# Last norm: the variance ahead of all but one subtraction, its sums in halves, and the last states' evictions as chains of their own

## The chip, the cores and the metric

The kernel runs on one core of a Trainium2 chip. The metric is the device time of one execution in microseconds, the median of several runs. Five engines work side by side, each through its own instructions in order: TensorE (PE, with its weight loads shown as PEld), VectorE (DVE), ScalarE (ACT), GpSimd (POOL) and SyncE (SP), which here only issues DMAs. They wait for each other through semaphores.

## The reference

One inference step of a decoder layer for 256 prompt tokens and 64 sample tokens (8 sequences of 8), 320 in all. Two token mixers run on the same input, their outputs are merged and projected, and two norms close the two halves of the layer:

```python
def _layernorm(x, g, b):
    mu = jnp.mean(xf, axis=-1, keepdims=True)
    var = jnp.mean(jnp.square(xf - mu), axis=-1, keepdims=True)
    return (xf - mu) * lax.rsqrt(var + LN_EPS) * g + b

x1 = LayerNorm(alpha * x + W_out(sig(g_a) * A(x) W_a + sig(g_b) * B(x) W_b))
y  = LayerNorm(alpha * x1 + relu(x1 W_up)^2 W_down)

C_new = decay * C + einsum('bhs,bhsk,bhsv->bhkv', w_end, k, v)      # mLSTM, 4 heads, 256 x 512
S_new = exp(G_end) * S + einsum('bhsk,bhsv->bhkv', k * exp(G_end - G), i)   # HGRN2, 8 heads, 128 x 256
```

The outputs are y and the new states. All is float32. The change touches the second norm (the one that gives y) and the last states of the prompt: C (4 heads, two blocks of 128x512 each) and S (8 heads, 128x256 each).

## The kernel before

Features lie on the partitions, in 16 blocks of 128, and the 320 tokens on the free axis. The whole layer is a list of 307 weight tiles of 2048 x 128. A tile is worked in two units of eight 128x128 weight blocks. Full precision is made from rounded numbers (float32r): a weight block w is split by ScalarE into a rounded half (`wh`) and by VectorE into the rest (`wl`), the moving operand likewise, and three matmuls hi*hi, hi*lo and lo*hi are accumulated, so a unit is 24 matmuls. Raw weights are loaded by SP into three buffers. The split halves have pairs of buffers: three narrow ones (`wh`, `wl`) and, from the output projection on, five wide ones in the tile `bb` (`wx[0]` to `wx[4]`). `prep` (L469) splits the next unit whenever a pair is free, and `give` (L544) hands a pair back when its unit is through; near the end it hands them to the last states' loads instead (`vx` for V halves, `kx` for K halves, loaded by GpSimd in `m_C`).

The order of the instructions on each engine is fixed when the program is built. Beside the main loop over weight tiles, each piece of side work is a chain: a Python generator that yields one operation at a time, with an estimated cost. A scheduler (`Sched`) keeps an estimated time for each engine. After each group of three matmuls it goes through all chains in order of rank (0 is first) and issues what its estimate says is ready, on the engine that the chain names. `wait` holds a chain for an event, `post` sets one, `acq` and `rel` take and return a buffer. Chips do not see these estimates: they only see the order that results.

The end of the program:

- The last 16 tiles (`dn`, f = 3) give the 16 blocks of the second norm's input; `ev_dn` (L1910) adds each to the residual in `acc` (the tile `f3m`). From block 4 on, a provisional mean `cb` of the first four blocks is subtracted first, so `ln_add` (L1722) waits for that mean after block 3.
- `ln_sum` keeps two sums over blocks, of z and of its square, one 128x320 tile each. The sum over the partitions is a matmul with a matrix of ones. In the first norm it is done by `total` (L1768), on halves that lie in the wide buffer `wx[4]` (`lns`, L606), which L1761 then returns to the weights. In the second norm it is a full-precision matmul: one after block 3, two after block 14 (`ln_pre`), two for block 15 itself (`ln_final`).
- `ln_scale` (L1807) gives the mean M, its square T, the variance X (L1816, L1819), logarithm and exponential, and a Newton step (L1822 to L1824).
- `y` (L1930) subtracts M from all 16 blocks (L1938) and multiplies them by the inverse deviation (L1943) on VectorE; `yb_` scales each by g and adds b on ScalarE, and stores blocks in pairs.
- `m_C` (L1098) and `h_S` (L1569) compute the C blocks and S heads on TensorE after the last tile. VectorE or ScalarE evicts them from PSUM (`oC`, `oS`), and SP stores them. They are chains of rank 3, and the eviction and store of a block belong to the chain that makes its sums.

Of the kernel before, what the change touches and what calls it, by code (L numbers as in the profile page):

```python
# [256 lines left out]
def post(ev):  # L257
    return ("set", ev)
# [47 lines left out]
class Program:  # L306
# [791 lines left out]
    def m_C(self, h):  # L1098
        k = yield acq(self.kx)
        kt = yield ("pool", 1000, lambda: self.nc.gpsimd.dma_start(k, self.kD[h]))  # L1100
        w = yield acq(self.vx)
        vt = yield ("pool", 1000, lambda: self.nc.gpsimd.dma_start(w, self.vD[h]))
        e = Ev()
        e.t = max(kt, vt) + 4000.0
        yield wait(e, self.main_end)
        for c in range(2):
            if h:
                yield wait(self.ln[1]["fin"])
            b = yield acq(self.mbank)
            yield ("pe", 6 * pe_r(512), lambda: [self.mm(  # L1110
                b, k[:, x, s, 128 * c:128 * c + 128], w[:, y, s, :], start=n == 0, stop=n == 5)
                for n, (s, x, y) in enumerate((s, x, y) for s in range(2) for x, y in ((0, 0), (0, 1), (1, 0)))])
            if c == 1:
                yield post(self.mh[h]["C"])
            if h < 2 and c == 0:
                yield ("dve", dve(512, True), lambda: self.nc.vector.tensor_copy(self.oC[h][:, c, :], b))
            else:
                yield ("act", act(512, True), lambda: self.A(self.oC[h][:, c, :], b))
            yield rel(self.mbank, b)
            yield ("sp", 620, lambda: self.dma(self.d["Cp"][h, :, c, :], self.oC[h][:, c, :]))  # L1120
        yield rel(self.vx, w)

# [446 lines left out]
    def h_S(self, h):  # L1569
# [7 lines left out]
            b[:, 0:256], x[:, 128 * i:128 * i + 128], x[:, 256 + 256 * i:512 + 256 * i], start=i == 0, stop=i == 1) for i in range(2)])  # L1577
        if h < 4:
            yield ("act", act(256, True), lambda: self.A(self.oS[:, h, :], b[:, 0:256]))
        else:  # L1580
            yield ("dve", dve(256, True), lambda: self.nc.vector.tensor_copy(self.oS[:, h, :], b[:, 0:256]))
# [140 lines left out]
    def ln_add(self, n, j, z, pre):  # L1722
# [4 lines left out]
        if j < 4:  # L1727
# [7 lines left out]
            if j == 3:  # L1735
                p = yield acq(self.sbank)
                if n == 0:
                    yield from self.total(p, S1, self.lns[0])
                else:
                    yield ("pe", pe_f(TOK), lambda: self.mm(p[:, :TOK], self.ones, S1, start=True, stop=True))  # L1740
# [16 lines left out]
        if j == 15:  # L1757
# [3 lines left out]
            self.hl_free.append((self.s.t["pe"], self.wx[4]))  # L1761
# [6 lines left out]
    def total(self, p, x, hl):  # L1768
        hi, lo = hl[:, 0, :], hl[:, 1, :]
        yield from self.split(x, hi, lo)  # L1770
        for i, y in enumerate((hi, lo)):
            yield ("pe", 147, lambda: self.mm(p[:, :TOK], self.ones.bitcast(F32R), y, start=i == 0, stop=i == 1))
# [14 lines left out]
    def ln_pre(self, n):  # L1787

        p = self.ln[n]["p"] = yield acq(self.sbank, 2)
        for i in range(2):  # L1790
            yield ("pe", pe_f(TOK), lambda: self.mm(p[i][:, :TOK], self.ones, self.lnb[i], start=True, stop=False))
# [15 lines left out]
    def ln_scale(self, n):  # L1807
# [11 lines left out]
        yield ("dve", dve(TOK, mode=2), lambda: v.tensor_scalar(X, X, 0.0, EPS, ALU.max, ALU.add))  # L1819
        yield ("act", act(TOK), lambda: self.A(RS, X, AF.Ln))  # L1820
# [109 lines left out]
    def y(self):  # L1930
# [4 lines left out]
        for i in range(KT + 6):  # L1935
# [3 lines left out]
            if i == 5:  # L1939
                yield wait(st["end"])  # L1940
            if i > 5:
                z = self.acc[:, i - 6, :]
                t = yield ("dve", dve(TOK), lambda: v.tensor_tensor(z, z, self.lnb[4], ALU.mult), (0.0,))  # L1943
                self.s.spawn(self.yb_(i - 6, z), 0, t)
# [9 lines left out]
    def run(self, pool):  # L1954
# [12 lines left out]
        self.ln = [dict(c=Ev(), end=Ev(), pre=Ev(), m=Ev(), fin=Ev(), s=[Ev() for _ in range(KT)]) for _ in range(2)]  # L1967
# [83 lines left out]
```

## Time and profile before

| | |
|---|---|
| median of 3 runs | 2321.09 us (2320.81 to 2322.24) |
| the profiled execution | 2321.41 us, span 2319.6 us |
| last accumulation of block 15 (L1918) | 2292.21 us from the span's start |
| ScalarE's last scaling of y ends | 2313.49 us |
| granted TensorE clock, mean | 0.999 |

The page gives the busy time of each engine in one profiled execution, and the trace behind it the start and length of each instruction. A row of the timeline is: start, length, engine, line, operation, out<-in, shapes and count, and in brackets how long the engine stood idle before it and what released it. The length of an operation is longer than its engine is occupied, since the next one can start before it ends: what an operation occupies is read from the starts. The line of a helper stands for all that it issues (L342 is every ScalarE operation, L348 nearly every matmul, L351 SP's DMAs), so one goes by the names of the tiles.

### The profile page before, as it was taken

How to read it: one execution, taken by the hardware profiler on the slowest of the kernel's cores; microseconds unless marked ns; L12 is line 12 of the kernel's file. 1: busy time of each engine (PE TensorE's matmuls, PEld its weight loads, DVE VectorE, ACT ScalarE, POOL GpSimd, SP SyncE). 2: the span in 40 equal slices, each digit the busy share in tenths (PEclk: the TensorE clock that was granted, in tenths of full speed). 3: DMA queues.
4: the chain of work that ended last, by engine and by line, in shares of the span. 5: the costliest groups of instructions: out<-in, count | busy, mean ns of one | idle time of the engine just before them, and what ended most of it. 6: DMA issues, size and time to landing. Idle time of an engine off the chain costs nothing.

```text
span 2319.6 us, 38982 instructions
## 1 busy us (share of the span) xinstructions
PE 2309.1 (100%) x15808; PEld 2267.0 (98%) x15808; DVE 1351.6 (58%) x2297; ACT 1059.5 (46%) x1703; POOL 11.9 (1%) x37
## 2 busy tenths in 40 slices
PE   9999999999999999999999999999999999999998
PEld 9999999999999999999999999999999999999997
DVE  6566567666666776555555767654444444444455
ACT  5444445555556565444433446533442343234333
POOL 0000000000000000000000000000000000000000
PEclk9999999999999999999999999999999999999999
DMA  7676777555555555555545654444444444444465
GB/s 282 206 254 223 269 280 230 193 187 181 183 181 188 182 189 172 174 177 169 176 169 176 213 167 152 150 146 154 146 155 146 154 147 154 146 153 147 153 219 182
DMA packets 143275, 424.92 MB, mean 183 GB/s; under 512 B 16372, under 2 KB 37748, under 8 KB 142072
## 3 DMA queue, kind: packets, MB, share of 16 engines
q1 hardware_dynamic: 141800, 415.96, 53.9%
q0 software_dynamic: 1152, 6.29, 0.8%
q8 instruction: 123, 2.02, 0.4%
q14 instruction: 56, 0.46, 0.1%
q10 hardware_dynamic: 144, 0.20, 0.0%
HBM read 371.48 MB, written 50.90 MB: 182 GB/s over the span
## 4 chain that ended last, share of the span: by engine, by line
PE 98%; ACT 1%; DVE 0%; DMA 0%; issue 0%; SPq 0%; ACTq 0%; DVEq 0%
PE bank L348 97%; ACT f3m L342 0%; DMA f<-first 0%; PE bank L1610 0%; PE bank L946 0%; PE bank L1175 0%; PE bank L1448 0%; DVE f3m L1938 0%; ACT f L342 0%; PE bank L1453 0%; PE bank L1019 0%; PE bank L1502 0%; PE bank L993 0%; PE bank L1559 0%; ACT oC L342 0%
## 5 line engine op out<-in xcount | busy, mean ns | idle before, releaser
L348 PE MATMUL bank<-xh,wh 128*128 128x320 f32 (+1 forms) x2432 | 782.4, 322 | 0.3 <-ACT wh L342 0.3
L488 DVE TENSOR_TENSOR wl<-wr,wh 128x1024 fp32r<-128x1024 f32 x426 | 522.0, 1225 | 399.6 <-ACT wh L342 395.9
L348 PE MATMUL bank<-xh,wl 128*128 128x320 f32 (+1 forms) x2432 | 752.2, 310 | 0.0
L348 PE MATMUL bank<-xl,wh 128*128 128x320 f32 (+1 forms) x2432 | 749.8, 309 | 0.0
L342 ACT ACTIVATE wh<-wr 128x1024 fp32r<-128x1024 f32 x426 | 451.0, 1059 | 498.1 <-PE bank L348 478.2
L348 PEld LDWEIGHTS bank<-xh,wh 128*128 128x128 f32 x2432 | 457.8, 188 | 19.2 <-issue 14.7
L348 PEld LDWEIGHTS bank<-xl,wh 128*128 128x128 f32 x2432 | 458.1, 189 | 2.9
L348 PEld LDWEIGHTS bank<-xh,wl 128*128 128x128 f32 x2432 | 458.0, 188 | 0.5 <-DVE wl L701 0.3
L488 DVE TENSOR_TENSOR bb<-wr,bb 128x1024 fp32r<-128x1024 f32 x176 | 215.7, 1226 | 229.2 <-ACT bb L342 229.1
L342 ACT ACTIVATE bb<-wr 128x1024 fp32r<-128x1024 f32 x176 | 186.4, 1059 | 313.3 <-PE bank L348 294.9
L348 PE MATMUL bank<-xh,bb 128*128 128x320 f32 (+1 forms) x1280 | 285.4, 309 | 0.0
L348 PE MATMUL bank<-rxb,bb 128*128 128x320 f32 x1208 | 276.3, 309 | 0.0
L348 PE MATMUL bank<-ra,wh 128*128 128x320 f32 x988 | 265.9, 308 | 0.0
L348 PE MATMUL bank<-ra,bb 128*128 128x320 f32 x1096 | 264.2, 308 | 0.7 <-DVE ra L1640 0.7
L348 PEld LDWEIGHTS bank<-xh,bb 128*128 128x128 f32 x1280 | 215.0, 188 | 0.0
L348 PEld LDWEIGHTS bank<-rxb,bb 128*128 128x128 f32 x1208 | 204.3, 188 | 0.2
L348 PE MATMUL bank<-xl,bb 128*128 128x320 f32 (+1 forms) x640 | 197.7, 309 | 0.0
L348 PEld LDWEIGHTS bank<-ra,bb 128*128 128x128 f32 x1096 | 187.1, 188 | 1.2 <-DVE ra L1640 0.9
L348 PEld LDWEIGHTS bank<-ra,wh 128*128 128x128 f32 x988 | 176.3, 188 | 0.0
L348 PE MATMUL bank<-rxb,wh 128*128 128x320 f32 x548 | 169.0, 308 | 0.0
L348 PE MATMUL bank<-rxb,wl 128*128 128x320 f32 x548 | 169.0, 308 | 0.0
L348 PEld LDWEIGHTS bank<-xl,bb 128*128 128x128 f32 x640 | 120.4, 188 | 0.3 <-DVE xl L1863 0.3
(263 smaller groups left out, 2233.9 us busy)
## 6 DMA issues: line engine op xcount, KB each, us to landing
wr<-wt SPq DMA_DIRECT2D x602, 512.0 KB, 3.4
rx<-C SPq DMA_DIRECT2D x34, 256.0 KB, 5.6
Cs<-rx SPq DMA_DIRECT2D x34, 256.0 KB, 4.4
f<-C SPq DMA_DIRECT2D x30, 256.0 KB, 5.3
Cs<-f SPq DMA_DIRECT2D x30, 256.0 KB, 4.8
f<-first SPq DMA_DIRECT2D x6, 704.0 KB, 10.8
vD<-ra SPq DMA_DIRECT2D x4, 1024.0 KB, 6.8
f<-S SPq DMA_DIRECT2D x8, 512.0 KB, 6.6
```

Source lines behind the costliest of these rows:

```text
L342: return self.nc.scalar.activation(out, in_, func, **kw)
L348: self.nc.tensor.matmul(*a, **kw)
L488: self.V().tensor_tensor(lo, raw, hi.bitcast(F32), ALU.subtract)
```

## The change

It does five things. (1) The second norm's sums over partitions go through `total`, in halves, where the sum can be made before block 15: one after block 3, two after block 14. `ln_final`'s two stay as they were. (2) For that, `wx[4]` is no longer returned after the first norm. (3) In `y`, VectorE subtracts from block 0 only, then waits for a new event `x` (the variance is made), subtracts from blocks 1 and 2, waits for the inverse deviation, and then alternates; before, it subtracted from six blocks ahead of that last wait, and nothing held the variance in front of them. (4) The eviction and store of each C block and S head become a chain of rank 0, spawned after its matmuls. (5) All C blocks are evicted by ScalarE; before, VectorE evicted the first blocks of heads 0 and 1. The second block of head 0 now waits for `fin` as well.

```diff
         for c in range(2):
-            if h:
+            if h or c:
                 yield wait(self.ln[1]["fin"])
...
-            if h < 2 and c == 0:
-                yield ("dve", dve(512, True), lambda: self.nc.vector.tensor_copy(self.oC[h][:, c, :], b))
-            else:
-                yield ("act", act(512, True), lambda: self.A(self.oC[h][:, c, :], b))
-            yield rel(self.mbank, b)
-            yield ("sp", 620, lambda: self.dma(self.d["Cp"][h, :, c, :], self.oC[h][:, c, :]))
+            self.s.spawn(self.C_out(h, c, b), 0, self.s.t["pe"])
         yield rel(self.vx, w)
+
+    def C_out(self, h, c, b):
+
+        yield ("act", act(512, True), lambda: self.A(self.oC[h][:, c, :], b))
+        yield rel(self.mbank, b)
+        yield ("sp", 620, lambda: self.dma(self.d["Cp"][h, :, c, :], self.oC[h][:, c, :]))
...
+        self.s.spawn(self.S_out(h, b), 0, self.s.t["pe"])
+
+    def S_out(self, h, b):
...
-                if n == 0:
-                    yield from self.total(p, S1, self.lns[0])
-                else:
-                    yield ("pe", pe_f(TOK), lambda: self.mm(p[:, :TOK], self.ones, S1, start=True, stop=True))
+                yield from self.total(p, S1, self.lns[0])
...
-            self.hl_free.append((self.s.t["pe"], self.wx[4]))
...
-    def total(self, p, x, hl):
+    def total(self, p, x, hl, stop=True):
         hi, lo = hl[:, 0, :], hl[:, 1, :]
         yield from self.split(x, hi, lo)
         for i, y in enumerate((hi, lo)):
-            yield ("pe", 147, lambda: self.mm(p[:, :TOK], self.ones.bitcast(F32R), y, start=i == 0, stop=i == 1))
+            yield ("pe", 147, lambda: self.mm(p[:, :TOK], self.ones.bitcast(F32R), y, start=i == 0, stop=stop and i == 1))
...
-            yield ("pe", pe_f(TOK), lambda: self.mm(p[i][:, :TOK], self.ones, self.lnb[i], start=True, stop=False))
+            yield from self.total(p[i], self.lnb[i], self.lns[1 + i], False)
...
         yield ("dve", dve(TOK, mode=2), lambda: v.tensor_scalar(X, X, 0.0, EPS, ALU.max, ALU.add))
+        if n:
+            yield post(st["x"])
...
-        for i in range(KT + 6):
+        for i in range(KT + 3):
...
-            if i == 5:
+            if i == 0:
+                yield wait(st["x"])
+            elif i == 2:
                 yield wait(st["end"])
-            if i > 5:
-                z = self.acc[:, i - 6, :]
+            if i > 2:
+                z = self.acc[:, i - 3, :]
                 t = yield ("dve", dve(TOK), lambda: v.tensor_tensor(z, z, self.lnb[4], ALU.mult), (0.0,))
-                self.s.spawn(self.yb_(i - 6, z), 0, t)
+                self.s.spawn(self.yb_(i - 3, z), 0, t)
```

What this does to the order is seen on three places. The first is VectorE behind the last accumulation into `f3m` (L1918 before, L1921 after), up to the first product. Names: `f_76` holds the norm's small tiles (M, T, X and the inverse deviation), `bank_87` and `bank_85` are C blocks, `bank_88` is the sum of squares. Before:

```order
L1918 TENSOR_TENSOR f3m<-f3m,bank_81 128x320
L1116 COPY oC<-bank_87 128x512
L1938 TENSOR_TENSOR f3m<-f3m,f_76 128x320 x6
L1816 SCALAR_TENSOR_TENSOR f_76<-bank_88,f_76 128x320
L1819 TENSOR_SCALAR f_76<-f_76 128x320
L1822 SCALAR_TENSOR_TENSOR f_76<-f_76 128x320
L1116 COPY oC<-bank_85 128x512
L1823 TENSOR_TENSOR f_76<-f_76 128x320
L1824 SCALAR_TENSOR_TENSOR f_76<-f_76 128x320
L1938 TENSOR_TENSOR f3m<-f3m,f_76 128x320
L1943 TENSOR_TENSOR f3m<-f3m,f_76 128x320
```

After:

```order
L1921 TENSOR_TENSOR f3m<-f3m,bank_81 128x320
L1941 TENSOR_TENSOR f3m<-f3m,f_76 128x320
L1817 SCALAR_TENSOR_TENSOR f_76<-bank_88,f_76 128x320
L1820 TENSOR_SCALAR f_76<-f_76 128x320
L1941 TENSOR_TENSOR f3m<-f3m,f_76 128x320 x2
L1825 SCALAR_TENSOR_TENSOR f_76<-f_76 128x320
L1826 TENSOR_TENSOR f_76<-f_76 128x320
L1827 SCALAR_TENSOR_TENSOR f_76<-f_76 128x320
L1941 TENSOR_TENSOR f3m<-f3m,f_76 128x320
L1948 TENSOR_TENSOR f3m<-f3m,f_76 128x320
```

The variance stands behind one subtraction instead of six and two copies of C are gone, one of them from between the Newton steps; three of the subtractions that stood in front now stand among the products.

The second place is ScalarE in the same stretch, from the square of block 15 to the first scalings of y (`f3m<-f3m,vec`). `bank_86` is the sum of z. Before:

```order
L342 ACTIVATE f_76<-f3m 128x320 x3
L342 ACTIVATE f_76<-bank_86 128x320 x2
L342 ACTIVATE oC<-bank_84 128x512
L342 ACTIVATE f_76<-f_76 128x320 x2
L342 ACTIVATE oC<-bank_82 128x512
L342 ACTIVATE oC<-bank_83 128x512
L342 ACTIVATE f3m<-f3m,vec 128x320 x2
L342 ACTIVATE oC<-bank_81 128x512
```

After:

```order
L342 ACTIVATE f_76<-f3m 128x320
L342 ACTIVATE oC<-bank_87 128x512
L342 ACTIVATE f_76<-bank_86 128x320 x2
L342 ACTIVATE f_76<-f_76 128x320
L342 ACTIVATE oC<-bank_84 128x512
L342 ACTIVATE f_76<-f_76 128x320
L342 ACTIVATE oC<-bank_85 128x512
L342 ACTIVATE oC<-bank_82 128x512
L342 ACTIVATE f3m<-f3m,vec 128x320
L342 ACTIVATE oC<-bank_81 128x512
```

Here `f_76<-bank_86 x2` are M and T, and `f_76<-f_76` are logarithm and exponential. The first C block is evicted ahead of M, and the second has moved from in front of the logarithm to between logarithm and exponential. After the first scaling four C evictions follow, before it were three.

The third place is VectorE in the last two tiles, where the last weights are prepared (L488) and blocks 13 and 14 accumulated (L1918 or L1921). Before:

```order
L488 TENSOR_TENSOR bb<-wr,bb 128x1024
L1918 TENSOR_TENSOR f3m<-f3m,bank_82 128x320
L1783 TENSOR_TENSOR f_76<-f_76,f3m 128x320
L1784 TENSOR_TENSOR f_76<-f_76 128x320
L1916 TENSOR_TENSOR f3m<-f3m,f_76 128x320
L1918 TENSOR_TENSOR f3m<-f3m,bank_83 128x320
L1783 TENSOR_TENSOR f_76<-f_76,f3m 128x320
L1784 TENSOR_TENSOR f_76<-f_76 128x320
L1916 TENSOR_TENSOR f3m<-f3m,f_76 128x320
```

After:

```order
L1921 TENSOR_TENSOR f3m<-f3m,bank_82 128x320
L1784 TENSOR_TENSOR f_76<-f_76,f3m 128x320
L1785 TENSOR_TENSOR f_76<-f_76 128x320
L488 TENSOR_TENSOR bb<-wr,bb 128x1024
L1919 TENSOR_TENSOR f3m<-f3m,f_76 128x320
L1921 TENSOR_TENSOR f3m<-f3m,bank_83 128x320
L1784 TENSOR_TENSOR f_76<-f_76,f3m 128x320
L1785 TENSOR_TENSOR f_76<-f_76 128x320
L1645 TENSOR_TENSOR bb<-f_76,bb 128x320 x2
L1919 TENSOR_TENSOR f3m<-f3m,f_76 128x320
```

The last unit's weights are prepared one tile later, behind the accumulation of block 13, and the rests of the two sums' halves (L1645) follow block 14.

More of the change, by code (lines that the diff above doesn't have):

```diff
@@ L1966, in run @@
         self.vD = [self.dr.tile([128, 2, 2, 512], F32, name=f"vD{j}") for j in range(MH)]
-        self.ln = [dict(c=Ev(), end=Ev(), pre=Ev(), m=Ev(), fin=Ev(), s=[Ev() for _ in range(KT)]) for _ in range(2)]
+        self.ln = [dict(c=Ev(), end=Ev(), pre=Ev(), m=Ev(), fin=Ev(), x=Ev(), s=[Ev() for _ in range(KT)]) for _ in range(2)]
         self.xq, self.xq_ev = [None] * KT, [Ev() for _ in range(KT)]
```

## The prediction

> **What bounds the kernel now.** I read the busy times first, then the waits of TensorE's own queue, then the chain that ended last, and only then the last 30 us in order of time.
>
> ```profile
> span 2319.6 us, 38982 instructions
> PE 2309.1 (100%) x15808; PEld 2267.0 (98%) x15808; DVE 1351.6 (58%) x2297; ACT 1059.5 (46%) x1703; POOL 11.9 (1%) x37
> ...
> PE bank L348 <- DVE ra L1640: 0.7, 1, 0.7
> PE bank L348 <- ACT wh L342: 0.3, 1, 0.3
> ```
>
> TensorE is busy from end to end; between the start and the last weight tile it waits 0.7 and 0.3 us. Up to there only TensorE's own work counts, and VectorE and ScalarE have room. The tail is another program: there TensorE's remaining sums are short, and the chain of waits runs through VectorE and ScalarE.
>
> ```profile
> 2295.02 2.09 DVE f3m L1938 x5
> 2297.11 0.41 DVE f L1816
> ...
> 2297.91 0.48 ACT f L342
> ...
> 2298.91 0.49 DVE f L1822
> 2299.41 0.60 DVE oC L1116
> ...
> 2301.33 0.40 DVE f3m L1943
> ...
> 2302.57 0.66 ACT f3m L342
> 2303.23 0.48 ACT oC L342
> ...
> 2308.05 0.54 ACT oS L342 x2
> ...
> 2312.40 1.09 ACT f3m L342 x2
> ```
>
> The columns are the start, the length and what. From 2295.02 five subtractions of the mean (L1938, behind a first one) stand ahead of the variance (L1816); logarithm, exponential and three small VectorE steps follow, with one copy of a C block (L1116) among them; the first product (L1943) comes at 2301.33. From 2302.57 ScalarE is never idle until 2313.49: 15 scalings of y, 3 evictions of C and 4 of S, which is 10.92 us. Behind it lie the stores.
>
> ```profile
> 2308.08 0.33 SPq L351 DMA_DIRECT2D y<-f3m  x1
> ...
> 2313.51 0.62 SPq L351 DMA_DIRECT2D y<-f3m  x1
> 2314.22 0.98 SPq L351 DMA_DIRECT2D Sp<-oS  x2
> SPq L2047 <- DMA Sp<-oS: 2.6, 1, 2.6
> 2308.00:2309.00 1.00, 1.00 (x6) 0.88 (x5) 1.00 (x4) 1.00 (x4) 0.00 (x0) 1.00 0.24 90
> 2309.00:2310.00 1.00, 1.00 (x6) 0.89 (x5) 1.00 (x3) 1.00 (x3) 0.00 (x0) 1.00 1.01 385
> 2314.00:2316.00 2.00, 0.00 (x0) 0.00 (x0) 0.00 (x0) 0.00 (x0) 0.00 (x0) 0.91 1.03 362
> 2317.00:2318.00 1.00, 0.00 (x0) 0.00 (x0) 0.00 (x0) 0.00 (x0) 0.00 (x0) 0.50 0.17 57
> ```
>
> The last store is issued at about 2314.7 and waited for 2.6 us. The last two columns of the stretches are the DMA share and GB/s: nearly idle in 2308 to 2309, then full from 2309 until, at 57 against 362 GB/s, the stream ends in the first sixth of 2317 to 2318, about 2317.2. The store issued at 2308.08 filled the engines from 2309.0 on, 0.9 behind its issue. So the end is ScalarE's last scaling, two issues, and a backlog of stores that began late. Everything is worked out on this execution, 2321.41 us (span 2319.6 and 1.8 around it); the median of the three runs is 0.3 lower.
>
> **The sums in halves.** Three full-precision sums of the last norm become a rounded half and a rest, two matmuls instead of one.
>
> ```profile
> 2209.29 0.31 PE L348 MATMUL bank<-rxb,bb 128*128 128x320 f32 x1
> 2209.44 0.70 PE L348 MATMUL bank<-f,ones 128*128 128x320 f32 x2
> ...
> 2210.12 0.31 PE L348 MATMUL bank<-ra,bb 128*128 128x320 f32 x1
> 1394.31 0.31 PE L348 MATMUL bank<-bb,ones 128*128 128x320 f32 x1
> 1394.46 0.31 PE L348 MATMUL bank<-xh,bb 128*128 128x322 f32 x1
> ```
>
> Matmuls are pipelined, so starts are what counts. A half occupies 0.15 (1394.31 to 1394.46, in the first norm). From 2209.29 to 2210.12, 0.83, pass two ordinary matmuls (0.30) and one full-precision sum: 0.53. Each sum therefore saves 0.53 - 0.30 = 0.23, three save 0.7 us, straight off the main stretch. The splits, three ScalarE and three VectorE operations of 0.5 each, cost nothing: two pairs lie in the last tile, where these rows show the cover, and the third in the middle of the stage.
>
> ```profile
> 2276.96 1.06 ACT L342 ACTIVATE bb<-wr 128x1024 fp32r<-128x1024 f32 x1 [2.46 <-PE bank L348]
> 2278.05 1.23 DVE L488 TENSOR_TENSOR bb<-wr,bb 128x1024 fp32r<-128x1024 f32 x1 [1.89 <-ACT bb L342]
> 2284.10 0.49 DVE L1918 TENSOR_TENSOR f3m<-f3m,bank 128x320 f32<-128x320 f32 x1 [2.99 <-PE bank L348]
> 2292.21 0.49 DVE L1918 TENSOR_TENSOR f3m<-f3m,bank 128x320 f32<-128x320 f32 x1 [6.14 <-PE bank L348]
> ```
>
> Ahead of the last accumulation VectorE idles 6.14 us; without that cover the two pairs would add their 2.0. The halves take buffer 4 of the wide weight buffers for good, so weights rotate through seven instead of eight pairs, and through three instead of four in the last nine units. A unit is 24 matmuls of 0.147, 3.5 us; its preparation runs from 2276.96 (the release) to 2279.28, 2.3 us, and about 0.3 for handovers. With three pairs a buffer is refilled two units, 7.1, ahead of use: 4.5 us of slack. In the last tile the only VectorE wait in front is the accumulation at 2284.10, and in the new order the last preparation stands ahead of it. I cost this at nothing; unhidden it is a unit's preparation, 2.6, per stall. The fourth V halves also now wait for the very last unit's buffer.
>
> ```profile
> 2288.41 0.54 POOL L1102 DMA_DIRECT2D bb<-vD  x1 [6.13 <-PE bank L348]
> DMA to landing us min/median/max: 5.2/7.6/9.7
> 2301.33 1.52 PE L348 MATMUL bank<-bb,wh 128*128 128x512 f32 x6
> ```
>
> Issued at about 2292.2 in place of 2288.41, they land between 2297.4 and 2301.9; the matmuls that read them start at 2301.33. On the median there are 1.5 us to spare; at worst 0.6 is lost, off the path since the last S copies have more than that. Zero.
>
> **The variance ahead of the subtractions.** All times here are on the old clock, before the 0.7. The variance needs the square of the mean and one subtraction now goes in front.
>
> ```profile
> 2293.60 0.69 DVE L1116 COPY oC<-bank 128x512 f32<-128x512 f32 x1 [0.90 <-PE bank L348]
> 2294.14 0.77 ACT L342 ACTIVATE f<-bank 128x320 f32<-128x320 f32 x2 [0.87 <-PE bank L348]
> 2296.07 0.60 ACT L342 ACTIVATE oC<-bank 128x512 f32<-128x512 f32 x1 [1.16 <-PE bank L348]
> 2308.49 2.90 DVE L1943 TENSOR_TENSOR f3m<-f3m,f 128x320 f32<-128x320 f32 x7
> 2309.22 1.89 PE L348 MATMUL bank<-xls 128*128 128x256 f32 x8
> 2311.30 1.41 DVE L1581 COPY oS<-bank 128x256 f32<-128x256 f32 x4
> ```
>
> Mean and square are done at 2294.91, so the variance starts at 2295.02 instead of 2297.11, 2.09 earlier; the logarithm, 0.80 behind it as before, at 2295.82, ending 2296.30. There the new order puts an eviction of C before the exponential. Its sums are done by 2296.07, so it does not wait, and it occupies ScalarE 0.48: the exponential ends at 2297.26 and L1822's step starts at 2297.28 instead of 2298.91, 1.63 earlier. The copy of 0.60 between the three steps is gone. Together 2.23: the first product at 2299.1, the first scaling at 2299.6. If that eviction had to wait, or the copy's place was idle anyway, 1.5 would remain. The new waits of the chains (for `x`, for `fin`) hold nothing else up: they set VectorE's order, shown above, and TensorE's order of the tail stays, but for two banks that change places.
>
> VectorE then has 13 subtractions and 16 products instead of 10 and 16. Its pitch is 0.40: the first product starts at 2301.3, the tenth, first of the last seven, at 2308.49, eighteen operations later. The three extra subtractions take back 1.2, and the last product starts near 2309.9; the four S copies behind it, 0.35 each (1.41/4), end near 2311.8, the last of them behind TensorE's last S sum at 2311.1 (2309.22 + 1.89).
>
> **Evictions.** The first C block is evicted by ScalarE before the mean: its sums end at 2293.60, where the copy on VectorE starts now; 0.48 later ScalarE is free at 2294.08, and the mean waits for TensorE until 2294.14. Nothing. After the first scaling stand 15 scalings, four C evictions (one more) and four S: 10.92 + 0.48 = 11.40, behind the first one's 0.55 (1.09/2), from 2299.6, which gives 2311.6 against 2313.49: 1.9 earlier. VectorE delivers a product each 0.80, and ScalarE needs per product 0.55 and half a C eviction, 0.79. So waits of a few tenths are possible: 1.4 as the lower bound.
>
> **Stores.** With the same issues behind the last scaling the end moves by those 1.9. But the backlog shrinks: the stores from the fifth C block on (four C and four S of 262 KB, y with 2.62 MB, 4.72 MB) are now issued evenly, from 2300.9 (one scaling and one eviction behind the first scaling's start, and the issue) to 2312.8 (the last scaling and the two issues of 0.71 and 0.49). At 362 GB/s they take 13.0; begun 0.9 behind the first issue, at 2301.8, they end at 2314.8 instead of 2317.2, 2.4 earlier. Between 1.9 and 2.4 I take 2.1. The Trainium skill (DMA: Bandwidth & Descriptors, Bandwidth) puts the HBM side of one core at about 358 GB/s and a single transfer of 1 MB at 341. The trace goes above the first (385 in a full stretch), so it does not cap here; by it the gain would be 2.2, by the second 1.6.
>
> Sum: 2321.41 - 0.7 - 2.1 = 2318.6, and 0.3 less for the median: **2318.3 us**, 0.12% below before.
>
> **Rivals.** First, ScalarE holds the gain back: it paces the tail already and gets two more evictions, one between logarithm and exponential. For it speaks that its demand equals VectorE's supply to a few hundredths; against, that all its C sums are ready early. If the tail gives only 0.5 to 1.2, the time is 2319.9.
>
> Second, slower: the eighth pair of weight buffers is missed. The place is the last nine units, with three pairs in rotation: a preparation that is held by more than 4.5 us behind another VectorE or ScalarE instruction stops TensorE. An accumulation that waits for a tile's end, up to 7 us, could do it; one such hold costs up to 2.5, and it makes the kernel slower than before from 2.8 in all, so two holds are needed: 2318.3 + 5.0 = 2323.3. For it: VectorE runs in order and its accumulations wait 3 to 6 us. Against: the preparations stand ahead of those waits in the order.
>
> Third, the variance moves but the end doesn't, since the stores or TensorE's last S sums (2311.1) set it. Then only the 0.7 remains: 2320.4. Against: TensorE's last sum is followed by 8.5 us today.
>
> Fourth, more: the last store alone would need 0.9 and 0.73 (262 KB at 362 GB/s) behind 2314.7, 2316.3, and the stream ends at 2317.2, so 0.9 of today's end is backlog. If all of it goes and ScalarE gives 2.1, the tail gains 3.0: 2317.4. For it speaks the even spacing; against, that the engines would be full nearly throughout.
>
> **How the numbers follow.** Forecast (2317.5 to 2319.3) 0.62; ScalarE holds back 0.14; stores or sums set the end 0.08; more gain 0.09; slower by stalls 0.07. The range that leaves out 2 in 10 at most, with the bounds 1.4 and 3.0 for the tail and a stall of one hold, is 2316.7 to 2321.4. A measurement of this kernel tells some 0.2%, 4.6 us, from no change. Faster than that, under 2316.4, needs a tail gain of 4, above every bound: 0.06. Slower, over 2325.7, needs three holds: 0.03. Within: 0.91.
>
> **What would show it.** In the profile after: full-precision sums of 128x320 left only in the tail (two, four records); the last accumulation 0.7 earlier; the variance directly behind one subtraction, within 0.5 of the mean's square; exponential 0.48 behind the logarithm's end with a C eviction between; first product about 2.9 earlier on the new clock; ScalarE without gaps to its last scaling at about 2310.9; stores full from about 2301 on, ending near 2314.3. Wrong would be: TensorE waits for wl or bb in the last 60 us, a gap on ScalarE between scalings above 0.3, or a last Sp store that waits as long as before although it is issued 2.6 earlier.

## The result and the profile after

The changed kernel takes 2317.77 us (median of 20 runs, 2317.18 to 2318.27), the kernel before 2321.10 in the same session (20 runs, 2320.28 to 2322.24): 3.33 us less, a ratio of 0.9985 with a 95% interval of 0.9979 to 0.9991. The profiled execution took 2317.66 us, with a span of 2315.7 against 2319.6.

The head of the page after, and the waits of TensorE's and SyncE's queues (total, times, longest):

```profile
span 2315.7 us, 38986 instructions
PE 2308.2 (100%) x15808; PEld 2267.3 (98%) x15808; DVE 1352.2 (58%) x2298; ACT 1062.1 (46%) x1708; POOL 12.0 (1%) x37
```

```profile
PE bank L348 <- POOL ones L631: 1.0, 1, 1.0
PE bank L348 <- DVE ra L1645: 0.7, 1, 0.7
...
SPq L2052 <- DMA Sp<-oS: 2.1, 1, 2.1
```

TensorE is as full as before and waits for no weight tile in the last stage. Before, the last wait, for the last S store, was 2.6.

The main stretch is compared by the accumulations on VectorE. The kernel before first (its rows at 2284.10 and 2292.21 stand in the prediction), then the changed one, with the halves of the last two sums on TensorE:

```profile
2206.12 0.49 DVE L1918 TENSOR_TENSOR f3m<-f3m,bank 128x320 f32<-128x320 f32 x1 [1.35 <-PE bank L348]
2229.86 0.48 DVE L1918 TENSOR_TENSOR f3m<-f3m,bank 128x320 f32<-128x320 f32 x1
```

```profile
2205.57 0.49 DVE L1921 TENSOR_TENSOR f3m<-f3m,bank 128x320 f32<-128x320 f32 x1 [1.35 <-PE bank L348]
2229.07 0.48 DVE L1921 TENSOR_TENSOR f3m<-f3m,bank 128x320 f32<-128x320 f32 x1
2283.31 0.49 DVE L1921 TENSOR_TENSOR f3m<-f3m,bank 128x320 f32<-128x320 f32 x1 [0.90 <-PE bank L348]
...
2289.55 0.30 PE L348 MATMUL bank<-bb,ones 128*128 128x320 f32 x1
2289.70 1.04 PE L348 MATMUL bank<-ra,bb 128*128 128x320 f32 x6
2290.58 0.31 PE L348 MATMUL bank<-bb,ones 128*128 128x320 f32 x1
...
2290.78 0.49 DVE L1921 TENSOR_TENSOR f3m<-f3m,bank 128x320 f32<-128x320 f32 x1 [4.52 <-PE bank L348]
```

2206.12 to 2205.57: this execution is 0.55 ahead before the first of the changed sums. It was 0.58 ahead at the first masked copy (435.7 to 435.1), where the two programs are still alike. The first sum adds 0.24 (2229.86 to 2229.07 is 0.79), and nothing happens until 2284.10 (2283.31, again 0.79). The two sums of the last tile make it 1.43, that is 0.64 for two. Two savings of 0.24 are 0.48; the other 0.15 is a half that now stands behind the last tile's matmuls (2290.58), so the accumulation is earlier by one half than the sum that the mean waits for.

The tail of the changed kernel in order of time:

```profile
2292.31 0.60 ACT L342 ACTIVATE oC<-bank 128x512 f32<-128x512 f32 x1 [0.48 <-PE bank L348]
2292.84 0.77 ACT L342 ACTIVATE f<-bank 128x320 f32<-128x320 f32 x2
2293.32 0.49 DVE L1941 TENSOR_TENSOR f3m<-f3m,f 128x320 f32<-128x320 f32 x1 [2.05 <-ACT f L342]
2293.72 0.48 DVE L1817 SCALAR_TENSOR_TENSOR f<-bank,f 128x320 f32<-128x320 f32 x1
...
2294.61 0.47 ACT L342 ACTIVATE f<-f 128x320 f32<-128x320 f32 x1 [0.99 <-DVE f L1820]
2294.98 0.58 ACT L342 ACTIVATE oC<-bank 128x512 f32<-128x512 f32 x1
2295.46 0.46 ACT L342 ACTIVATE f<-f 128x320 f32<-128x320 f32 x1
...
2297.82 0.48 DVE L1948 TENSOR_TENSOR f3m<-f3m,f 128x320 f32<-128x320 f32 x1
2298.34 0.66 ACT L342 ACTIVATE f3m<-f3m,vec 128x320 f32<-128x320 f32 x1 [0.23 <-DVE f3m L1948]
...
2304.20 1.22 ACT L342 ACTIVATE f3m<-f3m,vec 128x320 f32<-128x320 f32 x2
2305.57 0.65 ACT L342 ACTIVATE f3m<-f3m,vec 128x320 f32<-128x320 f32 x1
...
2308.28 2.29 ACT L342 ACTIVATE f3m<-f3m,vec 128x320 f32<-128x320 f32 x4
2309.08 1.41 DVE L1586 COPY oS<-bank 128x256 f32<-128x256 f32 x4
2309.50 1.42 SPq L351 DMA_DIRECT2D y<-f3m  x3
2311.02 0.94 SPq L351 DMA_DIRECT2D Sp<-oS  x2
```

One subtraction, then the variance; a C eviction between logarithm and exponential; the first product comes 7.04 behind the last accumulation (9.04 before). ScalarE's last scaling ends at 2310.57, 19.79 behind the last accumulation (21.27 before), and the last store is issued by 2311.96. The stretches of the tail, with the DMA share and GB/s in the last two columns:

```profile
2302.00:2304.00 2.00, 2.00 (x11) 1.71 (x10) 2.00 (x6) 2.00 (x5) 0.00 (x0) 1.00 0.98 366
...
2306.00:2308.00 2.00, 2.00 (x11) 1.77 (x10) 2.00 (x6) 2.00 (x6) 0.00 (x0) 1.00 0.82 309
...
2312.00:2313.00 1.00, 0.00 (x0) 0.00 (x0) 0.00 (x0) 0.00 (x0) 0.00 (x0) 1.00 1.01 344
2313.00:2314.00 1.00, 0.00 (x0) 0.00 (x0) 0.00 (x0) 0.00 (x0) 0.00 (x0) 0.81 0.68 240
```

From 2302 on the least filled stretch, 2306 to 2308, has a share of 0.82 (0.71 in its first microsecond); the nearly empty microsecond that stood at 2308 to 2309 before is gone. By the share of its last microsecond the stream ends near 2313.7, 22.9 behind the last accumulation (before 25.0). The landing that SyncE waits for comes a little later, at 2314.2, 23.4 behind (before 2317.9, 25.7).

So, on the traces: start of the execution 0.55 to 0.6, the same code and no part of the change; the main stretch 0.85; ScalarE's last scaling 1.48; behind it 0.99 (6.12 to 5.13). The last three make 3.32, which is what the medians show.

### The profile page after: what moved, and what is told of

Same layout as the page of the kernel before. It is cut to its first block, busy times and chain, and to the rows that moved or that the text cites. A ratio compares the mean times of both kernels' runs of the same rounds, so it can differ in the third digit from the quotient of the medians.

```text
span 2315.7 us, 38986 instructions
## 1 busy us (share of the span) xinstructions
PE 2308.2 (100%) x15808; PEld 2267.3 (98%) x15808; DVE 1352.2 (58%) x2298; ACT 1062.1 (46%) x1708; POOL 12.0 (1%) x37
## 3 DMA queue, kind: packets, MB, share of 16 engines
q8 instruction: 123, 2.02, 0.4%
## 4 chain that ended last, share of the span: by engine, by line
PE 99%; DVE 0%; ACT 0%; issue 0%; ACTq 0%; POOL 0%; DVEq 0%; POOLq 0%
PE bank L348 98%; PE bank L1615 0%; PE bank L946 0%; PE bank L1176 0%; DVE f3m L1941 0%; DVE f3m L1948 0%; PE bank L1449 0%; ACT f3m L342 0%; PE bank L1454 0%; PE bank L1019 0%; PE bank L1503 0%; PE bank L993 0%; PE bank L1560 0%; ACT f L342 0%; ACT oS L342 0%
## 5 line engine op out<-in xcount | busy, mean ns | idle before, releaser
L348 PE MATMUL bank<-xh,wh 128*128 128x320 f32 (+1 forms) x2504 | 804.9, 322 | 0.0
L488 DVE TENSOR_TENSOR wl<-wr,wh 128x1024 fp32r<-128x1024 f32 x440 | 539.1, 1225 | 438.2 <-ACT wh L342 434.5
L348 PE MATMUL bank<-xh,wl 128*128 128x320 f32 (+1 forms) x2504 | 774.4, 310 | 0.0
L348 PE MATMUL bank<-xl,wh 128*128 128x320 f32 (+1 forms) x2504 | 772.1, 309 | 0.0
L488 DVE TENSOR_TENSOR bb<-wr,bb 128x1024 fp32r<-128x1024 f32 x162 | 198.5, 1226 | 194.3 <-ACT bb L342 193.9
L348 PE MATMUL bank<-xh,bb 128*128 128x320 f32 (+1 forms) x1136 | 253.9, 309 | 0.0
L348 PE MATMUL bank<-rxb,bb 128*128 128x320 f32 x1088 | 249.0, 308 | 0.0
L348 PEld LDWEIGHTS bank<-xh,bb 128*128 128x128 f32 x1136 | 191.0, 188 | 0.0
L348 PE MATMUL bank<-rxb,wl 128*128 128x320 f32 x608 | 187.5, 308 | 0.0
L348 PEld LDWEIGHTS bank<-rxb,bb 128*128 128x128 f32 x1088 | 184.2, 187 | 0.0
L348 PE MATMUL bank<-xl,bb 128*128 128x320 f32 (+1 forms) x568 | 175.5, 309 | 0.0
L348 PE MATMUL bank<-bb,wh 128*128 128x320 f32 (+1 forms) x536 | 119.0, 313 | 0.0
```

The lines of the kernel that those rows point to most:

```text
L348: self.nc.tensor.matmul(*a, **kw)
L488: self.V().tensor_tensor(lo, raw, hi.bitcast(F32), ALU.subtract)
```

## The experiments

Every kernel below has the rest of its code as before or as changed; the kernel before, run beside them, had medians of 2321.01 to 2321.22. The four times are those of its profiled execution, behind the last accumulation: first product, end of ScalarE's last scaling, end of the last store's issue on SyncE, end of the span.

| kernel | median us (11 runs) | ratio to before, 95% interval | product | scaling | issue | end |
|---|---|---|---|---|---|---|
| before | 2321.10 (20) | 1 | 9.04 | 21.27 | 22.99 | 27.39 |
| before, again | 2321.42 | 1.0001 (0.9992 to 1.0010) | 9.04 | 21.26 | 22.98 | 27.59 |
| changed | 2317.77 (20) | 0.9985 (0.9979 to 0.9991) | 7.04 | 19.79 | 21.18 | 24.92 |
| sums in halves only | 2320.21 | 0.9995 (0.9987 to 1.0004) | 9.18 | 21.40 | 23.15 | 27.44 |
| seven pairs only | 2320.23 | 0.9997 (0.9988 to 1.0006) | 9.04 | 21.26 | 22.94 | 26.70 |
| order of y only | 2319.53 | 0.9993 (0.9984 to 1.0002) | 7.36 | 19.82 | 21.56 | 25.83 |
| evictions only | 2321.60 | 1.0002 (0.9993 to 1.0011) | 8.90 | 21.65 | 23.06 | 27.88 |
| changed, old evictions | 2318.85 | 0.9991 (0.9982 to 1.0000) | 7.52 | 20.00 | 21.94 | 26.20 |
| changed, evictions held | 2317.72 | 0.9986 (0.9977 to 0.9994) | 6.70 | 19.45 | 20.84 | 24.60 |
| the same, square first | 2317.17 | 0.9983 (0.9974 to 0.9992) | 6.50 | 19.25 | 20.66 | 24.35 |
| the same, S by GpSimd | 2317.31 | 0.9984 (0.9975 to 0.9992) | 6.51 | 19.27 | - | 24.40 |
| before, half of C stored | 2321.07 | 0.9999 (0.9990 to 1.0008) | 9.04 | 21.27 | 23.09 | 27.45 |
| changed, half of C stored | 2317.80 | 0.9986 (0.9977 to 0.9995) | 7.04 | 19.80 | 21.19 | 24.85 |
| before, half of S stored | 2319.91 | 0.9996 (0.9987 to 1.0005) | 9.04 | 21.28 | 22.70 | 26.40 |

**The kernel before, once more** (no edit).

> The kernel before, unchanged, profiled a second time, to tell spread of executions from spread of programs. The median must be 2321.0 to 2321.1. In the first profile the landmark (first masked copy) stands at 435.7 and the closing handshake behind the last store's landing takes 1.1 to 1.2; in the other kernels 434.9 to 436.2 and 0.7 to 1.3. If these belong to the execution, they come out different now; if they belong to the program, they come out as before within 0.1, and then the 0.8 by which the kernel with the withheld pair was faster is a matter of the program's placement and not of its buffers.

The median came out 0.3 above what was expected, so a median of 11 runs is good to some 0.4; with intervals of 0.0009 to either side of the ratio, that is 2 us, single parts of this change can't be read from times alone. The trace can: accumulation to product, scaling and issue repeat to 0.02. The first masked copy stood at 435.8 (435.7), and the end 4.61 behind the last issue (4.40): the first did not move, the second did, so this run alone did not settle the question. For the start, all runs together speak for the execution: the copy stands at 434.5 to 436.2 in them, though all programs are alike up to there. Counted from that copy, the spans differ from the span of the kernel before by what the medians do, within 0.25; the one exception is the changed kernel with held evictions (3.7 against 3.3).

**Sums in halves only.**

```diff
-                if n == 0:
-                    yield from self.total(p, S1, self.lns[0])
-                else:
-                    yield ("pe", pe_f(TOK), lambda: self.mm(p[:, :TOK], self.ones, S1, start=True, stop=True))
+                yield from self.total(p, S1, self.lns[0])
...
-            yield ("pe", pe_f(TOK), lambda: self.mm(p[i][:, :TOK], self.ones, self.lnb[i], start=True, stop=False))
+            yield from self.total(p[i], self.lnb[i], self.lns[1 + i], False)
...
-            self.hl_free.append((self.s.t["pe"], self.wx[4]))
```

> The kernel before with the first part alone: the three full-precision sums of the last norm in halves, and buffer 4 of the wide weight buffers kept for them (seven pairs, three at the end). My theory: 0.7 to 0.85 us faster than before (about 2320.3), all of it in TensorE's stretch: the last accumulation 0.7 to 0.85 earlier against the landmark at 2151, the tail behind it as long as before (27.4). The rival that the missing pair stalls TensorE: a wait for wl or bb in the last 60 us and the kernel 1.7 us slower or more. If the splits were not hidden, up to 2.0 would be added instead, so 1.2 slower.

```profile
2205.36 0.49 DVE L1914 TENSOR_TENSOR f3m<-f3m,bank 128x320 f32<-128x320 f32 x1 [1.35 <-PE bank L348]
...
2290.56 0.49 DVE L1914 TENSOR_TENSOR f3m<-f3m,bank 128x320 f32<-128x320 f32 x1 [4.52 <-PE bank L348]
```

From the first of these rows to the second, 85.20 against 86.09: 0.89, the same as in the changed kernel. The first product then stands 9.18 behind, 0.14 later than before: the half behind the last tile. TensorE waits for no weights. The sums are worth 0.7 net, and the median moved by 0.84.

**Seven pairs only** (the last line of that diff alone).

> The kernel before with nothing changed but the eighth pair of weight buffers withheld from the last norm on (the sums stay in full precision, nothing uses the buffer). My theory: no difference (0.0, within 0.2 us), no TensorE wait for weights, the fourth V halves 3.6 later. The rival of the missing pair: 2.5 us slower for each hold.

```profile
2291.76 0.53 POOL L1102 DMA_DIRECT2D bb<-vD  x1 [6.68 <-PE bank L348]
```

The last V halves are fetched later, as forecast (4.1 against the last accumulation, 3.6 were expected), and nothing up to the last issue differs (9.04, 21.26, 22.94): the missing pair stalls nothing. Yet the median is 0.8 lower, which was not expected. Its trace is 1.4 shorter than that of the kernel before. Of this, 0.7 is there at the first masked copy already, and 0.7 lies behind the last issue (3.76 to the end, against 4.40 and 4.61): 0.3 ahead of the last store's landing, the rest behind it. What makes that piece shorter stays open; it is the size by which all statements on the last 4 us of single traces are uncertain.

**Order of y only.**

```diff
-        for i in range(KT + 6):
+        for i in range(KT + 3):
-            if i == 5:
+            if i == 0:
+                yield wait(st["x"])
+            elif i == 2:
                 yield wait(st["end"])
-            if i > 5:
-                z = self.acc[:, i - 6, :]
+            if i > 2:
+                z = self.acc[:, i - 3, :]
...
+        if n:
+            yield post(st["x"])
```

> The kernel before with the third part alone: the variance behind one subtraction instead of six, products three behind the subtractions instead of six; evictions as before (two C blocks by VectorE, evictions and stores in their old chains), sums in full precision. My theory: the order is the main part of the tail's gain: 1.5 to 2.1 us faster (2319.0 to 2319.6), last accumulation where it was. Rival, the stores or the last S sums set the end: 0.0 to 0.3 faster. Rival, ScalarE holds it back: 0.5 to 1.2 faster.

```profile
2300.41 1.19 ACT L342 ACTIVATE f3m<-f3m,vec 128x320 f32<-128x320 f32 x2
...
2308.35 3.44 ACT L342 ACTIVATE f3m<-f3m,vec 128x320 f32<-128x320 f32 x6
2312.46 1.07 SPq L351 DMA_DIRECT2D Sp<-oS  x2
```

1.5 less, at the lower end of what was expected. ScalarE's last scaling ends 19.82 behind the accumulation: the order alone brings as much there as the whole change (19.79). The halves take 0.2 of it back and the evictions return them, as the kernel with the old evictions shows below (20.00). The rival that stores or sums hold the end is out: the end of the trace moves by 1.56.

**Evictions only** (the first two hunks of the change: C and S evictions and stores as chains of rank 0, all C blocks by ScalarE).

> The kernel before with the other parts alone: C and S evictions and their stores as chains of first rank, all C blocks by ScalarE; order of y and sums as before. My theory: these move no end by themselves, since a C eviction of 0.48 comes ahead of the exponential while the copy of 0.60 between the Newton steps goes, and ScalarE has one more eviction behind the first scaling: between 0.3 faster and 0.5 slower. Rival, the even spacing of the stores brings the gain: 0.9 faster or more.

```profile
2312.65 0.63 ACT L342 ACTIVATE oS<-bank 128x256 f32<-128x256 f32 x2
2313.18 1.19 ACT L342 ACTIVATE f3m<-f3m,vec 128x320 f32<-128x320 f32 x2
2314.82 0.96 SPq L351 DMA_DIRECT2D Sp<-oS  x2
```

No gain alone, and 0.5 more time, at the edge of what was expected: ScalarE ends 0.38 later (21.65), with one more C eviction behind the first scaling and two S evictions ahead of the last two scalings.

**The changed kernel with the old evictions** (halves and order).

> The changed kernel without its eviction parts: sums in halves and the new order of y, but C and S evictions and stores inside their old chains, the first C blocks of heads 0 and 1 copied by VectorE. If the parts add up as run alone (0.84 and 1.52 faster), it takes 2318.7 us, 0.9 slower than the changed kernel, and the eviction parts, which cost 0.5 alone, are worth 0.9 beside the new order: the copy of 0.60 between the Newton steps comes back, and the first scaling waits behind more C evictions. Rival, the eviction parts bring nothing: 2317.8, as the changed kernel. In the trace I expect ScalarE's last scaling to end 19.8 to 19.9 behind the last accumulation, as in the changed kernel, and the difference behind it.

```profile
2306.74 0.65 ACT L342 ACTIVATE oS<-bank 128x256 f32<-128x256 f32 x2
2307.27 2.83 ACT L342 ACTIVATE f3m<-f3m,vec 128x320 f32<-128x320 f32 x5
2307.96 2.51 SPq L351 DMA_DIRECT2D y<-f3m  x4
2308.88 1.40 DVE L1581 COPY oS<-bank 128x256 f32<-128x256 f32 x4
2310.51 1.53 SPq L351 DMA_DIRECT2D Sp<-oS  x3
```

2318.85: the halves and the order nearly add up (0.84 and 1.52 alone, 2.16 together), and the evictions that cost 0.5 alone are worth 1.1 beside the new order (1.28 in the traces). The rows show a part of it. ScalarE has evicted the second pair of S heads by 2307.4, but SyncE takes four stores of y first, and three S stores stand behind the last of y; in the changed kernel two do, and the second pair leaves ahead of the last three of y. ScalarE's end differs by only 0.21, the last issue by 0.76, the end by 1.28. The place of that store is not the whole of it. In the kernel before and with the order alone it is ahead of the last three of y, too; yet with the order alone the last landing is still 0.67 behind that of the changed kernel (24.08 against 23.41 behind the accumulation), while ScalarE ends at the same place (19.82 and 19.79). There the first scaling starts at 8.45 instead of 7.56, so the same scalings and stores stand closer together. That would be the even spacing of the prediction; no run separates it.

**Evictions held behind the exponential, and the square first.** One event more, posted behind the exponential, on which all C evictions but the first wait; in the second kernel the mean's square also goes ahead of the mean, and the subtractions wait for the variance.

```diff
     def C_out(self, h, c, b):
+        if h or c:
+            yield wait(self.ln[1]["e"])
...
         yield ("act", act(TOK), lambda: self.A(RS, RS, AF.Exp, scale=-0.5))
+        if n:
+            yield post(st["e"])
...
+        yield ("act", act(TOK, True), lambda: self.A(T, p1, AF.Square, scale=1.0 / D))
         t = yield ("act", act(TOK, True), lambda: self.A(M, p1, scale=1.0 / D))
-        st["m"].t = t
-        yield ("act", act(TOK, True), lambda: self.A(T, p1, AF.Square, scale=1.0 / D))
         yield ("dve", dve(TOK, True), lambda: v.scalar_tensor_tensor(X, p2, 1.0 / D, T, ALU.mult, ALU.subtract))
+        st["m"].t = t
```

> The changed kernel with one wait more: all C evictions but the first stay behind the exponential of the last norm (one event, posted behind it). The eviction of 0.48 leaves the place between logarithm and exponential, so the first product comes 0.4 to 0.5 earlier behind the last accumulation (7.04 there now). Theory, VectorE's alternation of 0.80 per product sets the end: 0.4 to 0.5 faster than the changed kernel, 2317.3. Rival, ScalarE's total sets it: the eviction is only put behind, 0.0 to 0.1 faster (2317.7). Rival, the stores or TensorE's last S sums set it: ScalarE's last scaling ends earlier by 0.4, the last store is issued earlier, but it waits longer, and the time stays at 2317.7.

> As the run with the held evictions, and the square of the mean is computed ahead of the mean, with the variance ahead of every subtraction: variance 0.36 to 0.40 earlier again, first product 0.8 to 0.9 earlier than in the changed kernel. If VectorE's alternation sets the end: 2316.9 to 2317.0. If ScalarE's total or the stores set it: 2317.6 to 2317.7, and the gap shows as ScalarE without any wait from the first scaling on, or as a longer landing of the last stores.

The second of the two:

```profile
2294.51 0.98 ACT L342 ACTIVATE f<-f 128x320 f32<-128x320 f32 x2 [0.73 <-DVE f L1822]
...
2297.45 0.48 DVE L1952 TENSOR_TENSOR f3m<-f3m,f 128x320 f32<-128x320 f32 x1
...
2307.91 2.29 ACT L342 ACTIVATE f3m<-f3m,vec 128x320 f32<-128x320 f32 x4
2310.65 0.96 SPq L351 DMA_DIRECT2D Sp<-oS  x2
```

The first product comes 0.34 and 0.54 earlier than in the changed kernel (0.4 to 0.5 and 0.8 to 0.9 were expected), and ScalarE's last scaling, the last issue and the end follow with nearly the same: 0.34 and 0.54, 0.34 and 0.52, 0.32 and 0.57. So in the traces the chain through VectorE's products still sets the end. The times say it less clearly. The median of the first kernel, 2317.72, did not move, where 2317.3 was expected and 2317.7 by the rivals; only its trace, from the last accumulation on, speaks for the theory. The second kernel is the fastest of all, 2317.17; its time alone does not part it from the changed one (the intervals overlap), the trace does by 0.57.

**The last S stores by GpSimd**, on top of that.

```diff
+            if h > 4:
+                yield ("pool", 1000, lambda: self.nc.gpsimd.dma_start(self.d["Sp"][q].rearrange("h p v -> p h v"), self.oS[:, q, :]))
+            else:
+                yield ("sp", 620, lambda: self.dma(self.d["Sp"][q].rearrange("h p v -> p h v"), self.oS[:, q, :]))
```

> The kernel with held evictions and the square ahead of the mean, and in addition the last two S stores issued by GpSimd instead of SyncE, where they stand behind the last two stores of y. If SyncE's line of issues behind the last scaling (1.4 there) sets the end, the last issue is that of y, 0.9 earlier, and the kernel takes 0.8 to 1.0 less than that one (2317.17): 2316.2 to 2316.4. If the stream of stores sets it, 0.3 to 0.4 less: 2316.8. Rival, GpSimd's stores land late, as its loads do (5 us and more behind the issue for 1 MB): then they are the last to land, and it takes 2318 or more.

```profile
2309.50 1.42 SPq L351 DMA_DIRECT2D y<-f3m  x3
...
2311.11 0.74 POOL L1593 DMA_DIRECT2D Sp<-oS  x1 [0.27 <-DVE oS L1588]
```

Nothing gained (2317.31, end 24.40 against 24.35). SyncE is done 1.0 earlier (19.62 behind the accumulation instead of 20.66), but GpSimd needs 0.7 per issue where SyncE needs 0.5, and its last store must wait for VectorE's last S copy, which ends 19.51 behind the accumulation in both kernels. So that store is issued 20.55 behind it, hardly earlier. All three numbers expected were missed.

**Half of the stores' bytes.** Three kernels store only half the columns of C or of S; the other half is left out of that output.

```diff
-            yield ("sp", 620, lambda: self.dma(self.d["Cp"][h, :, c, :], self.oC[h][:, c, :]))
+            yield ("sp", 620, lambda: self.dma(self.d["Cp"][h, :, c, 0:256], self.oC[h][:, c, 0:256]))
...
-            yield ("sp", 620, lambda: self.dma(self.d["Sp"][q].rearrange("h p v -> p h v"), self.oS[:, q, :]))
+            yield ("sp", 620, lambda: self.dma(self.d["Sp"][q].rearrange("h p v -> p h v")[:, :, 0:128], self.oS[:, q, 0:128]))
```

> The kernel before, with only the first 256 of the 512 columns of each C block stored (half of C is left out of the output, 1.05 MB less to store, of it 0.52 MB from the fifth block on; the number of stores and all arithmetic stay). It asks whether the backlog of stores sets the end behind ScalarE. Theory: ScalarE's last scaling still ends 21.27 behind the last accumulation, but the last store is issued 1.4 instead of 1.72 behind that, and lands as soon as a store alone can (0.9 and 0.73), so the transfers end 0.6 to 0.7 earlier than 24.96, and the kernel takes 2320.2 to 2320.5. Rival, issue and landing are fixed costs: no change, 2321.0 to 2321.4.

> The changed kernel with the same half of C left out of the stores. Theory: there the last store is issued 21.18 behind the last accumulation and the transfers end 1.7 later, which is what one store alone needs; no backlog is left, so the end moves by 0.0 to 0.2 only (2317.6 to 2317.8). Rival, the stream, which is full from 2302 to 2313 there, sets the end: 0.6 to 0.8 faster (2317.0 to 2317.2).

> The kernel before, with only the first 128 of the 256 columns of each S block stored (half of S is left out of the output, 0.52 MB in four stores, all among the last nine; number of stores and arithmetic stay). With half of C left out nothing moved, so if a backlog sets the end, it is that of the last nine stores alone, 2.37 MB from the hole at 2308 to 2309 on. Theory: ScalarE's last scaling ends 21.27 behind the last accumulation as before, the transfers end 0.5 to 0.8 earlier than 24.96, close to the last issue, and the kernel takes 2320.3 to 2320.6. Rival, the last issue and a fixed landing set the end: 2321.0 to 2321.4, with the transfers' end moved by less than 0.2.

The stretches of the kernel before (second profile), then with half of C, then with half of S stored:

```profile
2308.00:2309.00 1.00, 1.00 (x6) 0.87 (x6) 1.00 (x4) 1.00 (x4) 0.00 (x0) 1.00 0.25 97
...
2316.00:2317.00 1.00, 0.00 (x0) 0.00 (x0) 0.00 (x0) 0.00 (x0) 0.00 (x0) 0.50 1.02 353
2317.00:2318.00 1.00, 0.00 (x0) 0.00 (x0) 0.00 (x0) 0.00 (x0) 0.00 (x0) 0.50 0.28 94
```

```profile
2316.00:2317.00 1.00, 0.00 (x0) 0.00 (x0) 0.00 (x0) 0.00 (x0) 0.00 (x0) 0.50 0.95 319
2317.00:2318.00 1.00, 0.00 (x0) 0.00 (x0) 0.00 (x0) 0.00 (x0) 0.00 (x0) 0.50 0.02 7
```

```profile
2315.00:2316.00 1.00, 0.00 (x0) 0.00 (x0) 0.00 (x0) 0.00 (x0) 0.00 (x0) 0.50 0.66 183
```

A megabyte less of C changes nothing, in either kernel: before, the theory failed, and the stream still ends 25.0 behind the accumulation. Half a megabyte less of S moves it to 24.1 (0.9, a little more than the 0.5 to 0.8 expected), the last issue 0.3 forward, the end to 26.40 (27.39 and 27.59), and the median to 2319.91, 1.25 under the kernel before of the same session (2321.16; the interval of the ratio reaches to 1.0005, so the trace carries this). So a backlog does stand behind ScalarE's end, but it is made by the last nine stores alone, y and S, 2.36 MB issued from 2309.70 on: begun at 2310.6, 0.9 behind the first issue, they need 6.5 us at 362 GB/s and end at 2317.1, where the trace has it (2317.2). The sum is not exact: with S halved it gives 23.5 behind the accumulation where the trace has 24.1; the row shown moved 183 GB/s at a share of 0.66, so the halved stores kept the engines busy at a lower rate. No run halves S in the changed kernel. The Trainium skill (DMA: Bandwidth & Descriptors, Bandwidth) puts the HBM side of one core at about 358 GB/s; by that figure the nine would need an estimated 6.6. The 362 of this trace lie close to it, though a single stretch goes above (385, 2309 to 2310 in the prediction).

## Why the prediction was right, and where it was not

**The total** was forecast at 2318.3 and came at 2317.77, inside the forecast's own range and 0.5 on the fast side: 3.33 gained for 2.8. That it came so near is in part luck: ScalarE's end brought 0.4 less than its term of 1.9, and the stores behind it brought 1.0 where the sum had 0.2 (2.1 less 1.9). The prediction took 4.6 us for the least that a measurement tells from no change; with 20 runs of each kernel the interval of the ratio, 0.9979 to 0.9991, leaves out 1.

**The sums** were sized right: 0.7 forecast, 0.24 a sum in the rows. The accumulation moved by more, 0.85, since a half now runs behind the last tile, and the mean gives that 0.14 back. The lost eighth pair costs nothing, and the later V halves cost nothing: shown by the kernel with seven pairs, up to the last issue.

**The variance** stands behind one subtraction. In the run of the order alone it came 2.02 earlier (2.09 forecast); with the halves the 0.14 goes off. The exponential starts 0.38 behind the logarithm's end, with a C eviction between, where 0.48 was forecast, and the copy that left VectorE's Newton steps is worth 0.48 (7.52 to 7.04) where 0.60 stood in the sum. The first product was forecast 2.9 earlier; it is 3.43, and without this execution's early start 2.88.

**ScalarE's end** is the term that was too large: 1.9 forecast, 1.48 measured. The 0.14 of the sums is in it, and the rest, nearly 0.3, are waits for products: from the first scaling's start to the last one's end it took 12.23, where the count of evictions and scalings gave 11.95. Most of it is one wait. The prediction had put ScalarE's need at 0.79 per product against VectorE's 0.80, with half a C eviction in each; but the last C eviction stands ahead of the eighth and ninth scaling (2304.20), the S evictions come behind the tenth, and so the tenth waits for its product: it starts 0.80 behind the ninth (2305.57), where 0.55 would do. From there ScalarE has no wait until its end, so the delay stays. The prediction had named waits of a few tenths as its lower bound; it should have taken them into the sum. The kernels with the held evictions show it: bring the products forward, and ScalarE's end follows one to one.

**The stores** were forecast to take the stream's end forward by 2.4 and the issue's by 1.9, so 2.1 for the tail; measured were 2.1 for the stream, 1.81 for the last issue and 2.47 for the tail as the trace has it. The size was near, the mechanism was not. The step that failed is the stream counted as 4.72 MB from the fifth C block on: in the kernel before, halving C does not matter and halving S does. The eviction parts were costed at nothing, but beside the new order they are worth 1.1: in part because the second S pair is stored ahead of the last three stores of y, in part perhaps because the stores stand farther apart.

By the fourth rival the backlog of 0.9 would go entirely. By that rival's own measure it does not: the last store is issued at 2311.5, alone it would land 0.9 and 0.73 later, at 2313.1, and the stream ends at 2313.7, so 0.6 is left. The 0.99 behind ScalarE's end divides in another way. A third lies ahead of the last issue's end (1.72 to 1.39 behind the scaling), nearly all of it in the issue of the last y store, which took 0.62 before and 0.33 after. Nearly half lies between that issue and the landing (2.70 to 2.23). The last 0.2 lie behind the landing (1.72 to 1.52), where the kernel with seven pairs had 1.36 with the same stores; whether they belong to the change stays open.

**The rivals** that ScalarE holds the tail to 0.5 to 1.2, that stores or S sums set the end, and that the missing pair stalls, are out by the runs of the order alone and of the seven pairs.

## What to carry to other kernels

Where two engines hand work to each other at nearly equal rates, go through the sequence rather than the average: where one engine's side work runs out, it waits for the other. Then ask which of them the end follows when its first operation moves. For stores at the end, count first those behind the last hole in the transfers, and look at the order in which they stand in the issuing queue: here a finished tile behind four unfinished ones was part of a loss of 1.1 us. Parts of a change can cost alone and pay together; a leave-one-out run beside the one-alone run shows it.

## What was not expected of the hardware

From the last issue to the end of the span, traces of kernels with the same stores differ by up to 0.85: 3.76 (seven pairs), 4.40 and 4.61 (before, twice). Halving the bytes of eight 256 KB stores moved no time at all, while halving four others took 1.0 to 1.2 off the tail of the trace. A store of S issued by GpSimd occupied its issuer 0.72 to 0.74, where SyncE's took about 0.5 from one start to the next.
